# Neighbourhood attention with the values in four tiles, the division on its outputs, and fewer passes in the pooling beside it

## The chip, the cores and the metric

The kernel runs on one core of a Trainium2 chip. Its time is the device time of one execution in microseconds, from runs that are repeated on the same core. Engines are named as in the profile: PE (TensorE; PEld is its weight load), DVE (VectorE), ACT (ScalarE), POOL (GpSimd) and SP (SyncE, which here issues nearly all DMAs, one after another). PE's granted clock is given as a share of its upper level, 2.4 GHz; the lower level is 1.2 GHz.

## What is computed

Two layers over 1024 latent tokens (a grid of 16 rows and 64 columns) and 256 context tokens, 1024 features wide, in fp32. Each layer projects the normalised tokens into four groups of 256 features: a gated linear attention, a neighbourhood attention, a state-space scan and a pooling; each is multiplied by a gate, and one output projection adds the result to the stream. The change touches the neighbourhood attention (four heads of 64 features; a query sees 8 x 16 neighbours and all context tokens) and the pooling. Cut to what matters:

```
s_win = einsum('bhrqd,bhrikd->bhrqik', qg, k_rows) + bias      # qg already scaled
s_ctx = einsum('bhrqd,bhnd->bhrqn', qg, kch)
p = softmax(concat([s_win, s_ctx], -1))
o = einsum('bhrqik,bhrikd->bhrqd', p_win, v_rows) + einsum('bhrqn,bhnd->bhrqd', p_ctx, vch)

def centred_mean(u, w):          # w = 2, 4, 8, 16, 64 features each
    lo, hi = clip(t - w//2, 0, n), clip(t - w//2 + w, 0, n)
    return (csum[hi] - csum[lo]) / (hi - lo)
out_i = (centred_mean(g_i, w_i) - g_i) @ w_pool[i]
```

In layer 2 the context tokens have no queries of their own.

## The kernel before

The kernel is traced into one list of instructions per engine by a scheduler that takes them by priority and readiness and inserts the waits; each engine, and SP's queue of DMAs too, then runs its list in order. A buffer is a slot of a named tile; a new tile of that name waits until the old one's last reader is done.

For each layer the stages follow each other: projections and linear attention, the scan, then `na`, the neighbourhood attention, with the pooling and (in layer 1) gate projections woven into it, then the output projection `out_tiles`. fp32 products are made of two halves: a tile `hi` rounded to the matmul's format and `lo`, the rest.

`na` runs over jobs. A job is a head and a block of 128 queries, of which there are ten (two of context, eight of the grid); layer 1 has 40 jobs, layer 2 has 32. For a job, `na_scores` multiplies queries and keys into the score bank `nS` (L1331), DVE adds the bias and takes the maximum (L1338), ACT takes the exponential into `naP` and its sum into a column of `nast` (L1343), DVE takes the reciprocal (L1345) and scales all of `naP` by it (L1346). Three jobs later `na_turn` turns `naP` on PE by blocks of 128 (L1376), and ACT and DVE split the result into `naPT`, hi and lo (L1382, L1383). Two jobs form a pair; for a pair `na_values` multiplies `naPT` by the values into the half of a PSUM bank `nT` (L1398): rows 0 to 63 take hi by the values' hi plus lo by hi, rows 64 to 127 hi by the values' lo. ACT copies the upper rows (L1400, `nat`), and one DVE pass adds both into the head's output `nay` (L1412). `nT` has three buffers, shared by turns, values and pooling.

`na_head` loads a head's keys, queries and values. The values `naV` are one tile of ten blocks with one buffer (L1302, 640 KB), so the next head's load waits for the last product of the head before.

`pooling` goes in pieces of 256 tokens and 128 features (ten in layer 1, eight in layer 2), one after every fourth job. Each loads its input `pu` (L1453) and its inverse counts `piv` (L1455, one buffer), POOL forms window sums (L1457 to L1463), multiplies by the counts in two halves (L1465, L1466) and subtracts the input (L1467); PE multiplies by the weights (L1476), ACT copies out, and SP stores (L1479). `out_early` loads and multiplies the first output tiles (L376, L377) on SP and POOL before attention ends.

The modulation vector `csil`, 34 columns by four, is made once at the start on DVE (L185) and stays in a tile for the whole program.

Of the kernel before, what the change touches and what calls it, by code (L numbers as in the profile page):

```python
# [12 lines left out]
F32 = mybir.dt.float32  # L13
F32R = mybir.dt.float32r
I32 = mybir.dt.int32
AF = mybir.ActivationFunctionType
ALU = mybir.AluOpType
# [5 lines left out]
SEQ = 1024  # L23
CTX = 256
NTOK = SEQ + CTX
# [14 lines left out]
NH = '11'  # L40
NRM = 0
PS0 = 0
# [19 lines left out]
PW = 256  # L62
# [7 lines left out]
class Kernel:  # L70
# [72 lines left out]
    def load_consts(self):  # L143
        nc, c, a = self.nc, self.const, self.a
# [15 lines left out]
        self.dG = [self.dram.tile([D, NTOK], F32, name=f"dG{l}") for l in range(DEPTH)]  # L160
        self.dY = [self.dram.tile([D, NTOK], F32, name=f"dY{l}") for l in range(DEPTH)]
        self.dX = self.dram.tile([NTOK, D], F32, name="dX")
        self.dU = [self.dram.tile([NTOK, 256], F32, name=f"dU{l}") for l in range(DEPTH)]
# [9 lines left out]
    def silu_c(self):  # L173

        nc, v = self.nc, self.nc.vector
        cc, th = (self.t([128, 8, 2], "cc", 2) for _ in range(2))
        nc.sync.dma_start(cc, self.a["cc"])
        nc.scalar.activation(th, cc, AF.Tanh, scale=0.5)
        v.scalar_tensor_tensor(th, th, 1.0, cc, op0=ALU.add, op1=ALU.mult)
        v.tensor_scalar(th, th, 0.5, None, op0=ALU.mult)  # L180

        self.csil = self.const.tile([128, 4, 34], F32, name="csil")
        v.memset(self.csil, 0.0)
        for i in range(2):
            v.tensor_copy(self.csil[:, :, 32 * i:32 * i + 2], th.rearrange("p (a b) n -> p a b n", b=2)[:, :, i])  # L185

    def modulation(self, l, pieces, raws, width, psum, pool, lag=1):
# [1097 lines left out]
    def na_head(self, l, h, last):  # L1285
        nc = self.nc
# [7 lines left out]
        for piece in range(2):  # L1294
            q0 = 0 if piece == 0 else 640
            qt = self.t([128, NTOK], "naQ", 2, dtype=F32R).rearrange("p (i n) -> p i n", i=2)
            o = CTX if last and piece == 0 else 0
            for half in range(2):
                nc.sync.dma_start(qt[64 * half:64 * half + 64, :, o:].bitcast(F32), self.dQ[l][rows, :, q0 + o:q0 + 640])
            Q.append(qt)  # L1300
        V = self.t([128, 10, 128], "naV", 1, dtype=F32R)
        nc.sync.dma_start(V.bitcast(F32), self.dN[l][:, h * 128:(h + 1) * 128].rearrange("(t p) e -> p t e", p=128))  # L1302
        if h % 2 == 0:
# [82 lines left out]
    def na_values(self, l, job0, job1, last):  # L1386
        nc = self.nc
        (h, K, Q, V, yst), qb, r0, _, _, shared, PT, rest, ps = job0
        o = ps[:, 256:512]

        both = [(b, s, 0, 256) for s, b in enumerate(shared, 5 - len(shared))]
        one = [(b, 0, 128 * a, 128) for a, b in rest]
        hi = [(V[:, b, :], o, 0, s, q, n) for b, s, q, n in both + one]
        lo = [(V[:, b, 0:64], o[0:64], 1, s, q, n) for b, s, q, n in both + one]
        todo = hi[:1] + lo[:1] + hi[len(both):] + lo[1:] + hi[1:len(both)]
        for i, (w, out, part, s, q, n) in enumerate(todo):
            x = PT[:, part, s].rearrange("p a q -> p (a q)")[:, q:q + n]
            nc.tensor.matmul(out[:, q:q + n], lhsT=w, rhs=x, start=(i == 0), stop=(i == len(todo) - 1))  # L1398
# [7 lines left out]
        if NRM:  # L1406
            for i, r in enumerate((r0, job1[2])):
                nc.tensor.transpose(ps[0:64, i * 128:(i + 1) * 128], r.to_broadcast([128, 64]), self.ident)
            nc.vector.tensor_tensor(t[0:64], o[0:64], t[64:128], ALU.add)
            nc.vector.tensor_tensor(yc, view(t[0:64]), view(ps[0:64, 0:256]), ALU.mult if NRM == 1 else ALU.divide)  # L1410
        else:
            nc.vector.tensor_tensor(yc, view(o[0:64]), view(t[64:128]), ALU.add)  # L1412
# [15 lines left out]
    def pooling(self, l, last):  # L1428
# [4 lines left out]
        wb, sc = wb[:, 0:256].rearrange("p (m n) -> p m n", m=2), wb[:, 256:258]  # L1433
        nc.sync.dma_start(sc, a["pool_sc"][l])
        nc.sync.dma_start(wb, a["pool_wb"][l].rearrange("m k n -> k m n"))
        PAD = 8
# [3 lines left out]
        for (t0, t1, lo, hi) in pieces:  # L1440
            n = t1 - t0
            W = n + 2 * PAD
            for m in range(2):
# [9 lines left out]
                nc.sync.dma_start(u[:, d0:d1], self.dP[l][m * 128:(m + 1) * 128, c0:c1])  # L1453
                iv = self.t([128, PW], "piv", 1)
                nc.sync.dma_start(iv[:, :n], a["pool_inv"][:, m, t0:t1])  # L1455

# [7 lines left out]
                rr, uu = s4[:, PAD:PAD + n], u[:, PAD:PAD + n]  # L1464
                gp.tensor_tensor(s4[0:64, PAD:PAD + n], s2[0:64, PAD:PAD + n], iv[0:64, :n], ALU.mult)  # L1465
                gp.tensor_tensor(s4[64:128, PAD:PAD + n], s4[64:128, PAD:PAD + n], iv[64:128, :n], ALU.mult)  # L1466
                gp.tensor_tensor(rr, rr, uu, ALU.subtract)  # L1467
                todo.append((m, t0, n, u, rr, wb, sc))
# [63 lines left out]
    def run(self):  # L1532
# [9 lines left out]
        for l in range(DEPTH):  # L1542
# [5 lines left out]
            with self.phase("mods", True) as pool:  # L1548
                psum = self.ps2
                pm = lambda: psum.tile([128, 512], F32, tag="pm", bufs=1, name=self.nm("pm"))  # L1550
                todo = ((1, (2,)),) if last else ((0, (2,)), (1, (1, 0)))
# [45 lines left out]
def _consts():  # L1597
# [40 lines left out]
    out["id32"] = np.tile(np.eye(32, dtype=f), (4, 1))  # L1638
    inv = np.zeros((128, 2, NTOK), f)
    for wi, w in enumerate((2, 4, 8, 16)):  # L1640
        for off, n in ((0, CTX), (CTX, SEQ)):
            t = np.arange(n)
            cnt = np.clip(t - w // 2 + w, 0, n) - np.clip(t - w // 2, 0, n)
            inv[64 * (wi % 2):64 * (wi % 2) + 64, wi // 2, off:off + n] = (f(1.0) / cnt.astype(f))[None]
    out["pool_inv"] = inv
# [96 lines left out]
```

## Time and profile before

| | |
|---|---|
| time, median of 3 | 1372.81 us (1372.37 to 1374.88) |
| profiled execution | 1372.72 us, span 1370.9 us |
| mean granted clock of PE | 0.974 |
| PE, PEld busy | 1252.5 us (91%), 1009.2 us (74%) |
| DVE, ACT, POOL busy | 913.4 us (67%), 582.7 us (43%), 202.8 us (15%) |
| scaling of `naP` on DVE (L1346, 128x640 and 128x512) | 33.6 us for 48 and 10.0 us for 16 |

The span runs from the first to the last instruction. A busy share over the whole span mixes stages with different limits; the stage in question is read by a table of windows, and what an engine waited for by the table of waits. A wait for several things is put down to the one that came last.

### The profile page before, as it was taken

The page shows a single profiled execution, that of the slowest core. Times are in us where ns is not written, and L with a number is a line of the kernel's source. Part 1 is how long each engine was busy: PE and PEld are TensorE (multiplying, and loading weights), DVE is VectorE, ACT ScalarE, POOL GpSimd, SP SyncE. Part 2 cuts the span into 40 slices and gives each one's busy share as a digit, 9 for nine tenths or more (in the row PEclk, how much of TensorE's full clock was granted, in tenths as well). Part 3 has the DMA queues.
Part 4 walks back from the last instruction along what each step waited for, and adds up shares of the span by engine and source line. Part 5 has one row for each costly group of instructions (what it writes and reads, how often), then busy time and mean ns, then how long its engine had stood idle before and what let it go on. Part 6 is the DMA issues. An engine that isn't in the chain of part 4 may idle for free. (4 is left out here: it accounts for less than half of the span.)

```text
span 1370.9 us, 20412 instructions
## 1 busy us (share of the span) xinstructions
PE 1252.5 (91%) x7102; PEld 1009.2 (74%) x7102; DVE 913.4 (67%) x2269; ACT 582.7 (43%) x1234; POOL 202.8 (15%) x218
## 2 busy tenths in 40 slices
PE   5799999999999999888989999999999989787897
PEld 2698967676777677777778989868767766666676
DVE  2778577546388658774875689596554884877383
ACT  2653433223333347653455642453323333665321
POOL 0100000001100024442410000000212100335220
PEclk9799999999999999999999999999999999989999
DMA  9446686752533277637742475975315434864662
GB/s 330 170 124 223 195 252 177 227 161 77 166 125 117 79 195 187 179 121 234 236 117 91 134 221 187 256 200 165 88 50 184 154 127 145 213 146 131 197 209 89
DMA packets 233846, 228.99 MB, mean 167 GB/s; under 512 B 47144, under 2 KB 196136, under 8 KB 233408
## 3 DMA queue, kind: packets, MB, share of 16 engines
q1 hardware_dynamic: 232144, 225.05, 54.4%
q10 hardware_dynamic: 1584, 2.49, 0.5%
q8 instruction: 59, 0.97, 0.3%
q14 instruction: 59, 0.48, 0.1%
HBM read 157.88 MB, written 69.62 MB: 166 GB/s over the span
## 5 line engine op out<-in xcount | busy, mean ns | idle before, releaser
L317 PE MATMUL pa<-ahi,wh 128*128 128x512 f32 (+1 forms) x664 | 172.3, 386 | 3.3 <-DVE stg L346 1.5
L317 PE MATMUL pa<-ahi,wl 128*128 128x512 f32 (+1 forms) x664 | 165.9, 378 | 0.1
L317 PE MATMUL pa<-alo,wh 128*128 128x512 f32 (+1 forms) x664 | 163.8, 377 | 0.3 <-PEq L1571 0.3
L317 PEld LDWEIGHTS pa<-ahi,wh 128*128 128x128 f32 x664 | 115.4, 192 | 28.5 <-issue 6.0
L317 PEld LDWEIGHTS pa<-alo,wh 128*128 128x128 f32 x664 | 115.8, 192 | 22.5 <-issue 4.7
L317 PEld LDWEIGHTS pa<-ahi,wl 128*128 128x128 f32 x664 | 114.3, 190 | 22.7 <-issue 5.6
L302 POOL TENSOR_TENSOR wl<-w,wh 128x1024 fp32r<-128x1024 f32 (+1 forms) x19 | 46.4, 2445 | 277.7 <-PE pa L317 177.2
L333 PE MATMUL pa<-wh,ahi 128*128 128x256 f32 (+1 forms) x480 | 79.5, 300 | 4.9 <-DVE ahi L260 3.9
L387 PE MATMUL po<-wx,ahi 128*128 128x512 f32 x312 | 79.1, 393 | 2.8 <-DVE stg L473 1.6
L301 ACT CAST wh<-w 128x1024 fp32r<-128x1024 f32 (+1 forms) x51 | 53.8, 1056 | 62.5 <-PE pa L317 39.6
L333 PE MATMUL pa<-wl,ahi 128*128 128x256 f32 (+1 forms) x480 | 79.4, 299 | 0.1
L333 PE MATMUL pa<-wh,alo 128*128 128x256 f32 (+1 forms) x480 | 77.2, 296 | 0.0
L333 PEld LDWEIGHTS pa<-wh,ahi 128*128 128x128 f32 x480 | 66.8, 194 | 10.1 <-issue 3.0
L387 PEld LDWEIGHTS po<-wx,ahi 128*128 128x128 f32 x312 | 58.8, 190 | 16.3 <-ACT ahi L379 2.0
L333 PEld LDWEIGHTS pa<-wl,ahi 128*128 128x128 f32 x480 | 67.5, 194 | 3.6 <-issue 2.5
L333 PEld LDWEIGHTS pa<-wh,alo 128*128 128x128 f32 x480 | 66.2, 193 | 3.3 <-issue 3.0
L1331 PE MATMUL nS<-naK,naQ 128*128 128x256 f32 (+1 forms) x272 | 57.6, 333 | 11.4 <-DVE nast L1338 6.6
L1398 PE MATMUL nT<-naPT,naV 128*128 128x256 f32 (+3 forms) x368 | 58.1, 298 | 9.9 <-DMA naV<-dN 9.2
L1338 DVE CUSTOM_DVE_ANT_0 naP<-nS,nab 128x640 f32<-128x640 f32 (+1 forms) x64 | 50.2, 785 | 18.7 <-PE nS L1331 13.8
L1398 PEld LDWEIGHTS nT<-naPT,naV 128*128 128x128 f32 (+1 forms) x368 | 49.6, 176 | 15.4 <-issue 7.7
L1376 PE MATMUL nT<-c_ident,naP 128*128 128x128 f32 x320 | 51.5, 286 | 9.4 <-DVE nay L1412 3.9
L1383 DVE TENSOR_TENSOR naPT<-nT,naPT 128x512 fp32r<-128x512 f32 (+1 forms) x104 | 56.2, 559 | 5.7 <-ACT naPT L1382 5.3
(396 smaller groups left out, 2550.5 us busy)
## 6 DMA issues: line engine op xcount, KB each, us to landing
w<-in_w_in_dram SPq DMA_DIRECT2D x41, 512.0 KB
wm<-in_w_mod_dram SPq DMA_DIRECT2D x32, 512.0 KB
s5R<-dR SPq DMA_DIRECT2D x16, 960.0 KB
xt<-in_tok_dram SPq DMA_DIRECT2D x20, 512.0 KB
wm<-in_w_mod_dram SPq DMA_DIRECT2D x8, 1024.0 KB
dR<-sp_R SPq DMA_DIRECT2D x16, 512.0 KB
dG<-stg SPq DMA_DIRECT2D x32, 256.0 KB
w<-in_w_out_dram SPq DMA_DIRECT2D x16, 512.0 KB
```

What stands on the lines that cost most here:

```text
L301: nc.scalar.copy(hi, raw)
L302: (next(engines) if engines else self.eng(2)).tensor_tensor(lo, raw, hi.bitcast(F32), ALU.subtract)
L317: nc.tensor.matmul(ps[:, :t1 - t0], lhsT=w(k), rhs=x[:, k, t0:t1], start=(i == 0), stop=(i == 23))
L333: nc.tensor.matmul(ps[:, :n], lhsT=x[:, k, t * 128:(t + 1) * 128], rhs=w(k), start=(i == 0), stop=(i == 23))
L387: self.nc.tensor.matmul(o, lhsT=x[:, k], rhs=m(k), start=first and i == 0, stop=last and i == len(todo) - 1)
L1331: nc.tensor.matmul(self.na_s[:, c * 128:(c + n) * 128], lhsT=Qb[:, i, :], rhs=K[:, b * 128:(b + n) * 128], start=(i == 0), stop=(i == 1))
L1338: v.tensor_tensor_reduce(P[:, 0:nk], ps, self.na_b[:, b0:b0 + nk], 1.0, -NEG, ALU.add, ALU.min, nm)
L1376: nc.tensor.transpose(ps[:, i * 128:(i + 1) * 128], P[:, c * 128:(c + 1) * 128], self.ident)
L1383: (nc.gpsimd if RLO == "p" and len(src) < 4 else nc.vector).tensor_tensor(lo, pv, hi.bitcast(F32), ALU.subtract)
L1398: nc.tensor.matmul(out[:, q:q + n], lhsT=w, rhs=x, start=(i == 0), stop=(i == len(todo) - 1))
```

## The change

- The values of a head are four tiles: `naVc` for the two context blocks (two buffers), `naVa`, `naVb`, `naVd` for three, two and three blocks of the grid (one buffer each), with four loads.
- `naP` is no longer scaled. The reciprocal of each job's sum is turned on PE, as a 128x64 broadcast column against the identity, into the other half of the pair's `nT` bank, ahead of the value products. DVE adds the two halves of the output into `nat` (64x256) and a second pass multiplies by the turned reciprocals into `nay`.
- The pooling keeps 17 columns of factors per feature half, loaded once per layer: eight for the first and eight for the last tokens, made by POOL on 64x8 strips where a piece has such an edge, and the constant 1/w. DVE does the multiplication by 1/w and the subtraction in one pass for each half of 64 features.
- `csil` is stored to DRAM at the start and loaded again in the stage of each layer that uses it, so its tile is not held between.

```
-NRM = 0
+NRM = 1
+        self.dC = self.dram.tile([128, 4, 34], F32, name="dC")
-        self.csil = self.const.tile([128, 4, 34], F32, name="csil")
+        self.csil = self.t([128, 4, 34], "csil", 1)
...
+        nc.sync.dma_start(self.dC, self.csil)
...
-        V = self.t([128, 10, 128], "naV", 1, dtype=F32R)
-        nc.sync.dma_start(V.bitcast(F32), self.dN[l][:, h * 128:(h + 1) * 128].rearrange("(t p) e -> p t e", p=128))
+        parts = ((0, 2, "naVc", 2), (2, 3, "naVa", 1), (5, 2, "naVb", 1), (7, 3, "naVd", 1))
+        V = {}
+        for b, n, tag, bufs in parts:
+            x = self.t([128, n, 128], tag, bufs, dtype=F32R)
+            nc.sync.dma_start(x.bitcast(F32), self.dN[l][b * 128:(b + n) * 128, h * 128:(h + 1) * 128].rearrange("(t p) e -> p t e", p=128))
+            V.update((b + i, x[:, i]) for i in range(n))
...
         todo = hi[:1] + lo[:1] + hi[len(both):] + lo[1:] + hi[1:len(both)]
+        if NRM:
+            for i, r in enumerate((r0, job1[2])):
+                nc.tensor.transpose(ps[0:64, i * 128:(i + 1) * 128], r.to_broadcast([128, 64]), self.ident)
         for i, (w, out, part, s, q, n) in enumerate(todo):
...
         if NRM:
-            for i, r in enumerate((r0, job1[2])):
-                nc.tensor.transpose(ps[0:64, i * 128:(i + 1) * 128], r.to_broadcast([128, 64]), self.ident)
             nc.vector.tensor_tensor(t[0:64], o[0:64], t[64:128], ALU.add)
             nc.vector.tensor_tensor(yc, view(t[0:64]), view(ps[0:64, 0:256]), ALU.mult if NRM == 1 else ALU.divide)
...
+        iv = self.t([128, 2, 17], "piv", 1)
+        nc.sync.dma_start(iv, a["pool_inv"])
...
-                iv = self.t([128, PW], "piv", 1)
-                nc.sync.dma_start(iv[:, :n], a["pool_inv"][:, m, t0:t1])
...
-                gp.tensor_tensor(s4[0:64, PAD:PAD + n], s2[0:64, PAD:PAD + n], iv[0:64, :n], ALU.mult)
-                gp.tensor_tensor(s4[64:128, PAD:PAD + n], s4[64:128, PAD:PAD + n], iv[64:128, :n], ALU.mult)
-                gp.tensor_tensor(rr, rr, uu, ALU.subtract)
+                for p, x in ((slice(0, 64), s2), (slice(64, 128), s4)):
+                    for c, w, there in ((PAD, 0, t0 == lo), (PAD + n - 8, 8, t1 == hi)):
+                        if there:
+                            gp.tensor_tensor(x[p, c:c + 8], x[p, c:c + 8], iv[p, m, w:w + 8], ALU.mult)
+                    nc.vector.scalar_tensor_tensor(rr[p], x[p, PAD:PAD + n], iv[p, m, 16:17], uu[p], op0=ALU.mult, op1=ALU.subtract)
...
+                self.csil = self.t([128, 4, 34], "csil", 1)
+                nc.sync.dma_start(self.csil, self.dC)
```

The scheduler's order follows. In SP's list of layer 2, around the loads of the third head, it read before (`naQ`, `naK` queries and keys, `nab` bias, `w` output weights, `pu` and `dY<-pu` the pooling's input and output):

```order
L1453 DMA pu_18073<-dP_107 128x272
L1293 DMA naK_18212<-dK_101 64x1280 x2
L1479 DMA dY_90<-pu_17934 128x256
L1231 DMA nab_17612<-in_na_bias_dram 128x256
L1455 DMA piv_18203<-in_pool_inv_dram 128x256
L1302 DMA naV_17956<-dN_97 128x10x128
L1453 DMA pu_18199<-dP_107 128x272
L1299 DMA naQ_18215<-dQ_99 64x2x384 x2
L1415 DMA dY_90<-nay_17632 64x1024
```

and reads now:

```order
L1308 DMA naVa_18002<-dN_98 128x3x128
L1233 DMA nab_17650<-in_na_bias_dram 128x256
L1490 DMA dY_90<-pu_17853 128x256
L1308 DMA naVb_18004<-dN_98 128x2x128
L1295 DMA naK_18260<-dK_102 64x1280
L1463 DMA pu_18125<-dP_108 128x272
L1295 DMA naK_18260<-dK_102 64x1280
L1308 DMA naVd_18006<-dN_98 128x3x128
L1233 DMA nab_17650<-in_na_bias_dram 128x256
L1490 DMA dY_90<-pu_17981 128x256
L1301 DMA naQ_18263<-dQ_100 64x2x384 x2
L1463 DMA pu_18250<-dP_108 128x272
```

The one load of values stood behind a load of counts; now it is four loads, of which three are in these rows, each with other loads and stores between, and no load of counts is among them.

In DVE's list of layer 2, around the second pair of the first head, it read before (ISA is the bias and maximum pass of L1338 with the row that reads its result):

```order
L1346 TENSOR_SCALAR naP_17745<-naP_17745,nast_17746 128x640
L1383 TENSOR_TENSOR naPT_17733<-nT_17773,naPT_17733 128x128
L1345 RECIPROCAL nast_17782<-nast_17782 128x1
L1383 TENSOR_TENSOR naPT_17787<-nT_17788,naPT_17787 128x4x128
L1346 TENSOR_SCALAR naP_17781<-naP_17781,nast_17782 128x640
L1338 ISA naP_17799,nast_17800<-nS_17618,nab_17612 128x512
L1338 ISA nast_17800 128x1
L1412 TENSOR_TENSOR nay_17632<-nT_17773,nat_17831 64x2x16x8
L1383 TENSOR_TENSOR naPT_17787<-nT_17834,naPT_17787 128x4x128
L1345 RECIPROCAL nast_17800<-nast_17800 128x1
L1383 TENSOR_TENSOR naPT_17787<-nT_17841,naPT_17787 128x256
```

and reads now:

```order
L1390 TENSOR_TENSOR naPT_17834<-nT_17835,naPT_17834 128x4x128
L1355 RECIPROCAL nast_17830<-nast_17830 128x1
L1345 ISA naP_17846,nast_17847<-nS_17656,nab_17650 128x512
L1345 ISA nast_17847 128x1
L1417 TENSOR_TENSOR nat_17878<-nT_17821,nat_17878 64x256
L1478 SCALAR_TENSOR_TENSOR ps_3784_17855<-ps_3783_17854,piv_17725,pu_17853 64x256
L1478 SCALAR_TENSOR_TENSOR ps_3784_17855<-ps_3784_17855,piv_17725,pu_17853 64x256
L1355 RECIPROCAL nast_17847<-nast_17847 128x1
L1418 TENSOR_TENSOR nay_17676<-nat_17878,nT_17821 64x2x16x8
L1390 TENSOR_TENSOR naPT_17834<-nT_17882,naPT_17834 128x4x128
L1390 TENSOR_TENSOR naPT_17834<-nT_17889,naPT_17834 128x256
```

The scalings of `naP` are gone; the pass that adds into `nat` is followed by the two pooling passes and a reciprocal before the pass that multiplies into `nay` and frees the bank `nT_17821`.

On PE, the products of one pair in the same layer, with the turns of the reciprocals (`nast`) in front, read now:

```order
L1487 MATMUL nT_18389<-ps_3836_18127,pwb_17723 128x256
L1405 MATMUL nT_18357<-c_ident,nast_18223 64x128
L1405 MATMUL nT_18357<-c_ident,nast_18242 64x128
L1408 MATMUL nT_18357<-naPT_18315,naVa_18002 128x256
L1408 MATMUL nT_18357<-naPT_18315,naVa_18002 64x256
L1408 MATMUL nT_18357<-naPT_18315,naVa_18002 128x128
L1408 MATMUL nT_18357<-naPT_18315,naVa_18002 64x256
L1408 MATMUL nT_18357<-naPT_18315,naVc_18000 64x256 x2
L1408 MATMUL nT_18357<-naPT_18315,naVa_18002 64x128
L1408 MATMUL nT_18357<-naPT_18315,naVa_18002 128x256
L1408 MATMUL nT_18357<-naPT_18315,naVc_18000 128x256 x2
```

The two turns come before the first product and behind the pooling's product of that piece; before, the pair began with the product 128x256.

## Rows read from the trace of the kernel before

**Rows 1.** The page's part 1: busy us (share of the span) xinstructions.

```profile
PE 1252.5 (91%) x7102; PEld 1009.2 (74%) x7102; DVE 913.4 (67%) x2269; ACT 582.7 (43%) x1234; POOL 202.8 (15%) x218
```

**Rows 2.** Windows, attention of both layers: length, busy us (x) by engine, clock, DMA.

```profile
496.00:612.00 116.00, 103.46 (x673) 86.28 (x671) 94.67 (x233) 76.64 (x183) 50.88 (x67) 1.00 0.65 173
1165.00:1271.00 106.00, 81.24 (x490) 67.72 (x490) 81.73 (x197) 64.15 (x152) 41.48 (x56) 0.91 0.62 159
1170.00:1210.00 40.00, 31.28 (x211) 25.53 (x212) 35.62 (x91) 28.61 (x68) 12.55 (x17) 1.00 0.81 200
1210.00:1230.00 20.00, 17.25 (x93) 15.27 (x93) 14.23 (x36) 11.29 (x27) 8.65 (x12) 0.74 0.48 123
1240.00:1250.00 10.00, 4.18 (x22) 3.29 (x21) 5.50 (x13) 3.96 (x9) 4.67 (x8) 0.89 0.67 195
```

**Rows 3.** Waits, 1165 to 1300 us: engine line <- releaser: total us, times, longest.

```profile
PEld nS L1331 <- DVE nast L1338: 10.5, 18, 1.5
...
PE nT L1398 <- DMA naV<-dN: 6.1, 3, 4.4
```

**Rows 4.** Chain, 1231 to 1249 us: start us, us, what.

```profile
1242.07 0.73 POOL ps L1466
1242.82 0.33 SPq L1455
1243.21 5.24 DMA naV<-dN
```

**Rows 5.** Waits, 490 to 620 us.

```profile
PE nT L1398 <- DMA naV<-dN: 3.1, 2, 2.4
```

**Rows 6.** Lines by shape, 1165 to 1300 us: xcount | busy us, mean ns | idle.

```profile
L1346 DVE TENSOR_SCALAR naP<-naP,nast 128x640 f32<-128x640 f32 x24 | 14.9, 622 | 0.4
...
L1467 POOL TENSOR_TENSOR ps<-ps,pu 128x256 f32<-128x256 f32 x8 | 6.4, 802 | 0.6
...
L1465 POOL TENSOR_TENSOR ps<-ps,piv 64x256 f32<-64x256 f32 x8 | 6.1, 757 | 0.6
...
L1466 POOL TENSOR_TENSOR ps<-ps,piv 64x256 f32<-64x256 f32 x8 | 6.0, 745 | 0.6
...
L1346 DVE TENSOR_SCALAR naP<-naP,nast 128x512 f32<-128x512 f32 x8 | 5.4, 676 | 0.1
```

**Rows 7.** Lines by shape, 490 to 620 us.

```profile
L1376 PE MATMUL nT<-c_ident,naP 128*128 128x128 f32 x168 | 26.6, 278 | 3.6 <-DVE nay L1412 1.9 <-DVE nast L1345 1.0 <-DVE naP L1346 0.6
...
L1346 DVE TENSOR_SCALAR naP<-naP,nast 128x640 f32<-128x640 f32 x24 | 18.7, 777 | 0.2
...
L1346 DVE TENSOR_SCALAR naP<-naP,nast 128x512 f32<-128x512 f32 x8 | 4.6, 579 | 0.1
...
L1346 DVE TENSOR_SCALAR naP<-naP,nast 128x256 f32<-128x256 f32 x8 | 2.8, 354 | 0.5
```

**Rows 8.** Lines by shape, DVE, whole span.

```profile
L1412 DVE TENSOR_TENSOR nay<-nT,nat 64x256 f32<-64x256 f32 x36 | 15.0, 417 | 21.3 <-ACT nat L1400 20.6
...
L824 DVE SCALAR_TENSOR_TENSOR s5y<-s5y,s5g 128x256 f32<-128x256 f32 x2 | 0.8, 424 | 1.9 <-ACT s5y L823 1.9
```

**Rows 9.** Line 1376, what its engine waited for: us in total, times.

```profile
  DVE nay L1412: 12.9, 29
```

**Rows 10.** Timeline, 3 to 6 us: start us, us, engine line op.

```profile
4.01 1.67 SPq L211 DMA_DIRECT2D wm<-in_w_mod_dram  x3
...
5.13 0.25 DVE L185 COPY csil<-cc 128x8 f32<-128x8 f32 x2
```

**Rows 11.** Lines 1346, 380 and 1412 by themselves: duration ns min/median/max.

```profile
L1346 DVE TENSOR_SCALAR naP<-naP,nast x72: 352/550/1617, 495.8 to 1260.5; 128x640 f32<-128x640 f32 x48, 128x512 f32<-128x512 f32 x16, 128x256 f32<-128x256 f32 x8
...
L380 DVE TENSOR_TENSOR alo<-yt,ahi x28: 412/684/1790, 640.0 to 1322.7; 128x512 fp32r<-128x512 f32 x24, 128x256 fp32r<-128x256 f32 x4
...
L1412 DVE TENSOR_TENSOR nay<-nT,nat x36: 416/417/419, 507.5 to 1271.8; 64x256 f32<-64x256 f32 x36
```

More of the change, by code (lines that the diff above doesn't have):

```diff
@@ L1392, in na_values @@
         one = [(b, 0, 128 * a, 128) for a, b in rest]
-        hi = [(V[:, b, :], o, 0, s, q, n) for b, s, q, n in both + one]
-        lo = [(V[:, b, 0:64], o[0:64], 1, s, q, n) for b, s, q, n in both + one]
+        hi = [(V[b], o, 0, s, q, n) for b, s, q, n in both + one]
+        lo = [(V[b][:, 0:64], o[0:64], 1, s, q, n) for b, s, q, n in both + one]
         todo = hi[:1] + lo[:1] + hi[len(both):] + lo[1:] + hi[1:len(both)]
+        if NRM:
+            for i, r in enumerate((r0, job1[2])):
+                nc.tensor.transpose(ps[0:64, i * 128:(i + 1) * 128], r.to_broadcast([128, 64]), self.ident)
         for i, (w, out, part, s, q, n) in enumerate(todo):
@@ L1638, in _consts @@
     out["id32"] = np.tile(np.eye(32, dtype=f), (4, 1))
-    inv = np.zeros((128, 2, NTOK), f)
+    inv = np.zeros((128, 2, 17), f)
+    t = np.r_[0:8, SEQ - 8:SEQ]
     for wi, w in enumerate((2, 4, 8, 16)):
[L1641 to L1644, printed above, removed]
+        cnt = np.clip(t - w // 2 + w, 0, SEQ) - np.clip(t - w // 2, 0, SEQ)
+        at = inv[64 * (wi % 2):64 * (wi % 2) + 64, wi // 2]
+        at[:, 0:16], at[:, 16] = w * (f(1.0) / cnt.astype(f)), 1.0 / w
     out["pool_inv"] = inv
```

## The prediction

> **What bounds the kernel now.** I read the engines' sums first, then tables by stage, then the waits and the chain inside the two attention stages. Over the whole span TensorE (PE) is busy 1252.5 us of 1370.9, DVE 913.4 [rows 1]. That is an average; the change touches almost only the neighbourhood attention, once per layer, so I cut those two stages out [rows 2]: layer 1 at 496 to 612 us, layer 2 at 1165 to 1271 us. They differ. In layer 1 gate projections fill the gaps and PE is busy 103.5 of 116 us; DVE 94.7. In layer 2 little filler is left: PE 81.2 of 106 us, DVE 81.7, and between 1170 and 1210 us, where nothing stalls, DVE has 35.6 of 40 us and PE only 31.3. There DVE sets the pace: the loads of the score weights wait 10.5 us in all for the DVE pass that frees the score banks [rows 3]. Behind that stretch come two holes. In 1240 to 1250 us PE has 4.2 of 10 us; in 1210 to 1230 us it is busy, but at a granted clock of 0.74 [rows 2].
>
> The holes have a cause in the chain [rows 4]: the second of POOL's multiplications by the inverse counts ends at 1242.8 us, only then can SP issue the next load of those counts (one buffer), and only behind that the one load of all values of the next head, which lands 5.24 us later. SP issues in order, so POOL's pace holds attention's loads. PE waits for the values 6.1 us in layer 2 [rows 3] and 3.1 us in layer 1 [rows 5].
>
> **The change, part by part.** The rows' own execution took 1372.72 us (span 1370.9 and 1.8 around it), beside a median of 1372.81: the sum can start from either.
>
> *Values in four tiles.* The single buffer is free only after the head's last product, so the load cannot be hidden. Now the context blocks have two buffers and the other tiles come free one or two query pairs before they are wanted (the order rows of SP show them spread out, among other loads). A pair lasts 106/16 = 6.6 us, the whole load took 5.24 [rows 4], a quarter of it should take less. I take the waits as gone: -6.1 in layer 2, -3.1 in layer 1. Bounds: nothing (the new loads wait on PE in SP's queue and delay the queries behind them), and -9.2. What is late next is the pooling input and the queries, which stand in the same queue.
>
> *Division on the outputs.* Removed: 32 scalings of P in layer 2, 14.9 + 5.4 = 20.3 us [rows 6], and 40 in layer 1, 18.7 + 4.6 + 2.8 = 26.1 us [rows 7]. Added on DVE: one more 64x256 pass per pair, which the present one prices at 0.417 us [rows 8], so 16 x 0.417 = 6.7 and 20 x 0.417 = 8.3 us. Added on PE: two turns per pair. The trace has no 64x128 turn; the nearest is the 128x128 one, 26.6 us for 168 or 0.158 us [rows 7]. I take that: 32 x 0.158 = 5.1 us and 40 x 0.158 = 6.3 us. Ends: 0, if they fall into idle PE, and the whole 11.4.
>
> *Shorter pooling.* 18 loads of counts become 2, so SP no longer waits for POOL there; that gain is already in the waits for values. POOL loses 757 + 745 + 802 ns per piece [rows 6] and gets a few 64x8 products, which cost nothing while POOL is busy 41.5 of 106 us [rows 2]. DVE gets two 64x256 passes per piece. Nearest row: a scalar_tensor_tensor of 256 elements at 0.424 us [rows 8], so 16 x 0.424 = 6.8 us in layer 2 and 20 x 0.424 = 8.5 in layer 1. At a stage's end, where the last piece is waited for, 2.30 us of POOL give way to 0.85 of DVE and two edge products: I take -1.1 in layer 2 and -1.0 in layer 1; ends -1.5 and +0.9, a piece held once by DVE's queue.
>
> DVE net: layer 2 -20.3 + 6.7 + 6.8 = -6.8; layer 1 -26.1 + 8.3 + 8.5 = -9.3.
>
> *What of this reaches the path.* In layer 2 DVE paces most of the stage, so I count 5 of the 6.8. PE has a quarter of the stage idle, so its 5.1 count 1.5. In layer 1 PE is 89% busy: of the 9.3 from DVE I count 3, but of PE's 6.3 more than half, 3.5.
>
> *What waits longer.* The bank with a pair's outputs is freed by the last DVE pass on it. Now that is the second pass, and the order rows of DVE show other work between the two (a pooling pair, a reciprocal). Queued behind it on PE are the turns of the next job, and behind those ACT and the splitting passes. Today these turns wait for that DVE pass 29 times, 12.9 us in all [rows 9]. One pass more on every pair is 15.0 us (the price of rows 8 times 36); zero if DVE, relieved, comes to it earlier. I take +2.5 in layer 2 and +2.0 in layer 1. The turns of the sums themselves stand ahead of the products and need only a reciprocal that is long done.
>
> *The rest.* The modulation vector moves through DRAM: one store and two loads. The store waits at the start for DVE's copies, which end at 5.38 us, and the second weight load is queued behind it, while today three go out within 1.67 us from 4.01 [rows 10]. I cost it at 0, since the first loads are still on their way then; at most it is 1.3 us, from about 4.5 us to the 5.8 at which the store is out. The clock: 20 us at 0.74 are 5.2 us of full-speed work lost [rows 2]; with fewer holes I take back 1.
>
> **Sum.** Layer 2: -6.1 - 5.0 - 1.1 + 1.5 + 2.5 = -8.2. Layer 1: -3.1 - 3.0 - 1.0 + 3.5 + 2.0 = -1.6. Clock -1.0. Together -10.8: 1372.7 - 10.8 = 1361.9, so 1362 us.
>
> **A rule against it.** The removed scaling ran 352 to 1617 ns, and a splitting pass with both inputs in SBUF 412 to 1790 ns, while the pass over PSUM and SBUF kept to 416 to 419 [rows 11]. So passes of the first kinds are held by something, and the two new pooling passes read two SBUF operands. The Trainium skill, "SBUF — State Buffer", section "Who interferes with whom", says that a DVE instruction with two SBUF inputs and a GpSimd instruction that reads SBUF exclude each other for the whole instruction. The spreads agree with it. By that rule the passes that go (2-port scalings) were victims as well, so it cuts both ways; only the rival below takes it at its worst.
>
> **Rivals.**
> *The larger gain.* Layer 2 drops to its engines' own work. PE 81.2 less 106 x 0.09 = 9.5 for the slow clock plus 5.1 is 76.8 us, DVE 81.7 - 6.8 = 74.9. At the 0.89 share that DVE holds in the undisturbed stretch the stage takes 76.8 / 0.89 = 86.3 us, 19.7 less than 106; layer 1 as PE-bound gains nothing: 1353 us. For it: both holes have one cause. Against: the chain leaves other loads late.
>
> *No change.* Each of the 36 new pooling passes is held by one POOL product (0.745 us, rows 6), 26.8 us on DVE; the net of -16.1 becomes +10.7. The 8 us counted for DVE are gone and some 3 come on top: 1361.9 + 11 = 1373 us. For it: the spreads. Against: POOL is left with about 41.5 - 18.4 = 23 us in 106, so a pass meets it one time in five.
>
> *Slower: the output bank held over two passes.* Place: the turns of the next job, in both layers. Price per pair 0.417 us, and 0.85 more where the pooling pair stands between the passes, which happens for up to 18 of the 36. With PE's 11.4 in full and the removed waits at -9.2 - 2.1 = -11.3 these two cancel, and if DVE's freed time stays unused, every delayed pair counts: half of them, 18 x 0.417 = 7.5, give 1380 us. It decides as soon as more than 10 pairs are held without DVE's gain. For it: 29 such waits today. Against: each of them is short (0.44 us), and DVE is what gets relieved.
>
> **How the numbers follow.** The forecast 0.56, the larger gain 0.20, no change 0.11, slower 0.13. A measurement of this kernel tells about 0.2%, 2.7 us. Faster by more than that: nearly all of the first two and a little of the third, 0.76; within: 0.11; slower: 0.13. The forecast's own range is 1355 to 1369; with the larger gain's lower end and the no-change case 1348 to 1375, which leaves out most of the slower case.
>
> **What would show it.** In the changed profile no matmul of values should wait for a load by more than about a microsecond; the stretch of layer 2's attention should be 7 to 11 us shorter and its clock nearer 1; the turns of the sums should be near 0.16 us of PE each; the waits of turns for the second output pass should stay under 18 us in all; layer 1's stage should be within 3 us of 116. I am wrong if PE's idle time in layer 2 stays near 25 us under another releaser (pooling, queries, the output pass), or if layer 1's stage grows by more than 3 us.

## The result, and the profile after

The changed kernel is slower: 1386.11 us median (1380.85 to 1390.71, 7 runs) beside 1372.37 (1370.91 to 1374.88, 7 runs) of the kernel before, a ratio of 1.0095 with a 95% interval of 1.0077 to 1.0114. My 1362 us is off by 24, and the result lies above the range (1348 to 1375).

The engines' sums of the profiled run (1388.17 us, span 1386.4) answer to [rows 1]:

```profile
PE 1252.4 (90%) x7174; PEld 1013.0 (73%) x7174; DVE 912.8 (66%) x2269; ACT 583.4 (42%) x1234; POOL 165.0 (12%) x188
```

PE and DVE do as much as before, POOL 38 us less, and the span is 15.5 us longer. The loss is idle time: PE has 134.0 us of it where it had 118.4. Windows of the same lengths as the attention stages in [rows 2], with the same columns, begun within 3 us of the first score product:

```profile
498.00:614.00 116.00, 103.43 (x670) 87.45 (x669) 84.57 (x218) 72.40 (x175) 25.45 (x46) 0.97 0.57 153
1180.00:1286.00 106.00, 80.06 (x520) 67.98 (x521) 78.29 (x196) 63.89 (x149) 23.51 (x40) 0.94 0.57 151
```

PE is idle for 25.9 of 106 us in layer 2, as before (24.8), but its releaser is another one. These are waits of the changed kernel, 1175 to 1288 us (engine line <- releaser: us in total, times, longest):

```profile
POOL ps L1465 <- DMA pu<-dP: 43.5, 4, 16.1
PEld nS L1338 <- DVE nast L1345: 23.0, 21, 4.3
...
PE nS L1338 <- DVE nast L1345: 17.2, 12, 4.1
```

The wait for values [rows 3] has gone; the load of the score weights waits 23.0 us for DVE's bias/max pass (L1345, formerly L1338) where it was 10.5. Over the whole span, the instructions that write the score bank `nS` wait for that pass so long (us, times), first in the kernel before, then in the changed one. Each sum counts the weight loads and the products, which in part wait at the same time; the line below it has PE's products alone, which wait 14.9 us more than before:

```profile
  DVE nast L1338: 22.7, 47
PE nS L1331 <- DVE nast L1338: 6.6, 13, 1.3
```

```profile
  DVE nast L1345: 54.1, 54
PE nS L1338 <- DVE nast L1345: 21.5, 16, 4.1
```

Why is DVE late at it, with less work? The changed kernel's chain (start us, us, what), then DVE, POOL and PE in order of time around it:

```profile
1225.97 3.64 DMA dY<-pu
...
1229.66 4.62 DMA pu<-dP
...
1234.45 0.65 POOL ps L1465
...
1235.16 0.64 POOL ps L1469
...
1235.87 0.64 POOL ps L1470
...
1236.54 1.04 DVE ps L1478
1237.58 0.03 issue
1237.62 0.48 DVE ps L1478
...
1238.13 0.82 DVE naP L1345
...
1239.02 1.43 PE nS L1338 x4
```

```profile
1234.78 0.42 DVE L1417 TENSOR_TENSOR nat<-nT,nat 64x256 f32<-64x256 f32 x1 [0.66 <-ACT nat L1410]
1236.54 1.56 DVE L1478 SCALAR_TENSOR_TENSOR ps<-ps,piv,pu 64x256 f32<-64x256 f32 x2 [1.35 <-POOL ps L1470]
1238.13 0.82 DVE L1345 CUSTOM_DVE_ANT_0 naP<-nS,nab 128x640 f32<-128x640 f32 x1
```

```profile
1236.58 0.72 POOL L1471 TENSOR_TENSOR ps<-ps 64x256 f32<-64x256 f32 x1
```

```profile
1239.02 1.43 PE L1338 MATMUL nS<-naK,naQ 128*128 128x384 f32 x4 [4.08 <-DVE nast L1345]
...
1247.44 0.59 PE L1487 MATMUL nT<-ps,pwb 128*128 128x256 f32 x2
```

Read it from the top: a finished pooling output is stored from `pu`; only then may the same buffer be loaded for a later piece; POOL sums it; the two new DVE passes need the sums; the next bias/max pass stands behind them in DVE's list; and PE needs that one before it writes the next scores. PE stands still for 4.08 us. Up to 2.9 of them, from the end of DVE's pass before (1234.78 + 0.42) to the bias/max pass, are the wait for POOL and the two passes, for a piece of pooling whose product PE multiplies at 1247.44. Before, POOL waited for `pu` as much, but alone; its waits over the whole span, in the kernel before and in the changed one:

```profile
POOL ps L1457 <- DMA pu<-dP: 65.7, 12, 14.1
```

```profile
POOL ps L1465 <- DMA pu<-dP: 53.9, 7, 16.1
```

### The profile page after: what moved, and what is told of

Same layout as the page of the kernel before. It is cut to its first block, busy times and chain, and to the rows that moved or that the text cites. A ratio compares the mean times of both kernels' runs of the same rounds, so it can differ in the third digit from the quotient of the medians.

```text
span 1386.4 us, 20596 instructions
## 1 busy us (share of the span) xinstructions
PE 1252.4 (90%) x7174; PEld 1013.0 (73%) x7174; DVE 912.8 (66%) x2269; ACT 583.4 (42%) x1234; POOL 165.0 (12%) x188
## 5 line engine op out<-in xcount | busy, mean ns | idle before, releaser
L319 PE MATMUL pa<-ahi,wl 128*128 128x512 f32 (+1 forms) x664 | 170.2, 382 | 0.0
L319 PE MATMUL pa<-alo,wh 128*128 128x512 f32 (+1 forms) x664 | 160.6, 374 | 0.3 <-PEq L1584 0.3
L1338 PE MATMUL nS<-naK,naQ 128*128 128x256 f32 (+1 forms) x272 | 59.2, 339 | 25.3 <-DVE nast L1345 21.5
L335 PE MATMUL pa<-wl,ahi 128*128 128x256 f32 (+1 forms) x480 | 76.6, 294 | 0.1
L1338 PEld LDWEIGHTS nS<-naK,naQ 128*128 128x128 f32 x272 | 41.7, 198 | 39.6 <-DVE nast L1345 32.6
L1350 ACT ACTIVATE naP<-naP,nast 128x640 f32<-128x640 f32 (+1 forms) x64 | 51.5, 805 | 28.2 <-DVE nast L1345 22.0
L348 DVE SCALAR_TENSOR_TENSOR stg<-stg,pa 128x512 f32<-128x512 f32 (+1 forms) x40 | 25.2, 631 | 50.2 <-ACT stg L347 46.8
```

The lines of the kernel that those rows point to most:

```text
L319: nc.tensor.matmul(ps[:, :t1 - t0], lhsT=w(k), rhs=x[:, k, t0:t1], start=(i == 0), stop=(i == 23))
L335: nc.tensor.matmul(ps[:, :n], lhsT=x[:, k, t * 128:(t + 1) * 128], rhs=w(k), start=(i == 0), stop=(i == 23))
L348: nc.vector.scalar_tensor_tensor(th[:, :t1 - t0], th[:, :t1 - t0], 1.0, ps, op0=ALU.add, op1=ALU.mult)
L1338: nc.tensor.matmul(self.na_s[:, c * 128:(c + n) * 128], lhsT=Qb[:, i, :], rhs=K[:, b * 128:(b + n) * 128], start=(i == 0), stop=(i == 1))
L1350: nc.scalar.activation(P[:, 0:nk], src, AF.Exp, bias=nm, scale=-1.0, accum_out=l1)
```

## The experiments

In their names the three digits say whether the values are in four tiles, the pooling passes on DVE, the division on the outputs; 111 is the change. All have the small table of counts, and all but `e_table` the stored `csil`. Ratios are against the kernel before on the same chip, with 95% intervals. "Layer 1" is the time from its first score product to its first output product, "layer 2" that from its last projection to the end, each from one profile (143.0 and 206.2 us before, 151.7 and 209.3 in the change), so that differences of two or three us are not read.

**One part undone.** Pooling passes back on POOL:

```diff
-                    nc.vector.scalar_tensor_tensor(rr[p], x[p, PAD:PAD + n], iv[p, m, 16:17], uu[p], op0=ALU.mult, op1=ALU.subtract)
+                    gp.tensor_tensor(rr[p], x[p, PAD:PAD + n], iv[p, m, 16:17].to_broadcast([64, n]), ALU.mult)
+                gp.tensor_tensor(rr, rr, uu, ALU.subtract)
```

> The changed kernel (1386.1 us) with the pooling passes off DVE again: POOL multiplies each half by its count and subtracts the input, out of the small table; the values in four tiles and the division on the outputs stay. Theory 1 (DVE's queue: the 36 pooling passes stand in DVE's list ahead of bias/max passes and wait there for POOL, and so for the load of `pu`; on the chain of layer 2's attention `pu` loads and L1478 hold some 7 us each): the wait of PE's score products for the bias/max pass falls from 54 us back to about 23, and the time to 1360 to 1368. Rival 2 (the division on the outputs is what costs: the 72 turns and the bank held over two passes): 1380 to 1386. Rival 3 (the four value loads hold up SP's queue): 1380 to 1386.

Division back on the probabilities (`NRM = 0`):

> The changed kernel with the division put back on the probabilities (72 scalings of naP on DVE, one output pass, no turns of the sums); values in four tiles and DVE's pooling passes stay. Theory 1 (DVE waits in its queue for the pooling sums): DVE gets some 20 us of scalings in each layer's attention and loses 7 us of output passes, and still waits for POOL, so no better than 1386, up to 1400. Rival 2 (the division on the outputs costs): 1368 to 1378.

One value tile again (`naV`, ten blocks, one load):

> The changed kernel with the values in one tile and one load a head again. Theory 1: the value waits of 6.1 us in layer 2 and 3.1 us in layer 1 come back, in part under the waits of DVE: 1386 to 1395. Rival 3 (four loads on SP, each held until PE gives its tile free, delay the loads of `pu` and queries behind them): 1372 to 1380.

Two of the three undone (the first edit, and `NRM = 0`):

> Only the values in four tiles (and, as in all these kernels, the small table of counts and `csil` stored and loaded again): scalings on the probabilities, pooling all on POOL. Theory 1: the value waits of the kernel before (9.2 us in both layers) go and about half of it shows, 1366 to 1370 against 1372.4 before. Rival 3 (the four loads are what cost): 1378 to 1386.

Measured: e101 0.9955 (0.9934 to 0.9977), e110 1.0037 (1.0016 to 1.0059), e011 1.0099 (1.0065 to 1.0133), e100 0.9929 (0.9902 to 0.9957). Taking the passes off DVE is worth 1.4% (19 us) with the division on the outputs and 1.1% (15 us) without. The wait for the bias/max pass falls from 54.1 to 32.3 us in e101, not to the 23 of the text. With the scalings that wait is the same with the passes on DVE (24.4 us, e110) and without (24.6, e100); there PE's products of the pooling wait 12.1 us where it was 5.1, so that the loss shows at another place of PE's list. The value tiles gain nothing while DVE stalls (1.0099 without them against 1.0095), so four loads in SP's queue are not what costs. e110 speaks against theory 1 as the only cause: that had said no gain, and it gained 0.6%, so the division on the outputs costs too. Its 1379.87 us lie just above rival 2's 1368 to 1378, its ratio within them (1.0037 of 1372.4 is 1377.5). e100 is a little faster than its text, which had not counted the small table.

**The other combinations.** The same edits, combined:

> Values in one tile and pooling all on POOL; of the change only the division on the outputs with its turns is left (and the small table, and `csil` stored and loaded). From the runs so far: taking DVE's pooling passes out was worth 1.4% with the values split (0.9955 against 1.0095), so theory 1 expects 0.996 to 1.000 here against 1.0099 with the passes. If the passes cost only together with the split values (their loads between those of `pu` in SP's queue), 1.005 to 1.010.

> None of the three parts: scalings on the probabilities, one tile of values, pooling on POOL; only the small table of counts (17 columns, loaded once a layer, with edge passes) and `csil` stored and loaded twice. All theories: 0.997 to 1.002 of before. If the trip of `csil` delays the gated stages, 1.002 to 1.004; if the small table's fewer loads on SP help by themselves, 0.993 to 0.997.

> The kernel before with only the small table of counts: one load a layer in the place of 18 of 128 KB, the edges multiplied by POOL apart, the rest by one number a row, still on POOL; `csil` stays in its tile. With `csil` moved as well it was 0.9959. If the table is the gain and the trip of `csil` costs nothing: 0.994 to 0.998. If the table gives nothing: 0.999 to 1.001.

Measured: e001 1.0008 (0.9992 to 1.0024), e000 0.9959 (0.9934 to 0.9985), e_table 0.9964 (0.9943 to 0.9985). e001 lies just above what was expected, e000 on the table's side: the small table alone gives 0.4%, and nothing shows that moving `csil` costs. The split values give 0.3% (e000 to e100), within its uncertainty of 0.4, and 0.5% (e001 to e101), clear of its 0.3; the division on the outputs costs 0.3 to 0.6% in three pairs, each uncertain by some 0.3.

**Wait or work?** The DVE passes with their shape and their place in the list, but no POOL to wait for, in the kernel with one value tile:

```diff
-                    nc.vector.scalar_tensor_tensor(rr[p], x[p, PAD:PAD + n], iv[p, m, 16:17], uu[p], op0=ALU.mult, op1=ALU.subtract)
+                    nc.vector.scalar_tensor_tensor(pd[p, :n], pd[p, :n], self.na_r[p], pd[p, :n], op0=ALU.mult, op1=ALU.subtract)
```

Here `pd` is a tile of ones and `na_r` the latest reciprocal. For the first 128 features POOL also forms its last sum on 128 rows instead of 64.

> The one-tile kernel with DVE's 36 pooling passes of the same shape and place in DVE's list, but on a tile of their own and the reciprocal just before them, so that they wait for no POOL and no load (PE then takes the plain window sums: the counts and the subtraction are left out of the output). Theory 1a (the wait in DVE's queue is what costs): near the kernel with pooling on POOL, 0.996 to 1.001 of before. Theory 1b (the DVE time itself, 36 passes of some 0.4 to 0.6 us on the loop score bank, bias/max pass, next scores): 1.005 to 1.010, as with the wait.

A third buffer for the pooling input:

```diff
-                u, s2, s4 = (self.t([128, PW + 2 * PAD], x, b) for x, b in (("pu", 2), ("ps2", 1), ("ps4", 2)))
+                u, s2, s4 = (self.t([128, PW + 2 * PAD], x, b) for x, b in (("pu", 3), ("ps2", 1), ("ps4", 2)))
```

> The one-tile kernel with DVE's pooling passes as in the change, but three buffers for `pu`, so that a piece's load no longer waits for the store of the piece two before. Theory 1a: POOL's wait for `pu` (89 us in all with one tile) falls by half or more, DVE's passes find their sums ready, 1.000 to 1.004 of before. Theory 1b: 1.007 to 1.010, no change from 1.0099.

Measured: e011_nowait 0.9920 (0.9891 to 0.9950), e011_pu3 1.0002 (0.9981 to 1.0023), against 1.0099 for e011. These are the passes (xcount | busy us, mean ns | idle before) of e011, of e011_pu3, and of e011_nowait:

```profile
L1475 DVE SCALAR_TENSOR_TENSOR ps<-ps,piv,pu 64x256 f32<-64x256 f32 x36 | 21.6, 600 | 21.1 <-POOL ps L1474 11.9 <-POOL ps L1467 4.7 <-POOL ps L1462 3.8
```

```profile
L1475 DVE SCALAR_TENSOR_TENSOR ps<-ps,piv,pu 64x256 f32<-64x256 f32 x36 | 21.7, 603 | 16.3 <-POOL ps L1474 8.2 <-POOL ps L1467 5.9 <-POOL ps L1462 1.0
```

```profile
L1478 DVE SCALAR_TENSOR_TENSOR pd<-pd,nast 64x256 f32<-64x256 f32 x36 | 18.9, 526 | 0.4
```

18.9 us of work stay on DVE, the 21.1 us of waiting go, and the kernel is 1.8% (24 us) faster: theory 1b, the passes' own time, had said 1.005 to 1.010. But the 24 us are not the price of the wait alone. The kernel is faster than either range of its text, and 0.9% faster than e001, which has no such passes on DVE at all. The edit also frees POOL's tiles earlier, and PE's products of the pooling need neither POOL's multiplications nor DVE's passes: they wait 2.3 us, where it was 7.1 in e011 and 9.1 in e001. The mended kernels below do without this edit. Earlier loads give 1.0% (13 us): they shorten DVE's wait (21.1 to 16.3 us), POOL's wait for `pu` falls from 89.5 to 70.3 us and not by half, and PE's products of the pooling wait no more.

**The whole change, mended.** The passes stand one pooling step later, tied to that step's reciprocal so that the scheduler can't pull them forward; first with the tiles of the change, then with three `pu` and one buffer for the context values, then that with the division on the probabilities:

```diff
...
+                if late:
+                    w = self.t([128, 1], "pw", 2)
+                    nc.vector.tensor_scalar(w, self.na_r, 0.0, late[0][2], op0=ALU.mult, op1=ALU.add)
+                    for p, o, x, y in late[1:]:
+                        nc.vector.scalar_tensor_tensor(o, x, w[p], y, op0=ALU.mult, op1=ALU.subtract)
+                late = [(0, 0, iv[:, m, 16:17])]
                 if len(todo) == PLAG:
...
-                    nc.vector.scalar_tensor_tensor(rr[p], x[p, PAD:PAD + n], iv[p, m, 16:17], uu[p], op0=ALU.mult, op1=ALU.subtract)
+                    late.append((p, rr[p], x[p, PAD:PAD + n], uu[p]))
...
```

The small pass into `w` multiplies the reciprocal by zero and adds the constant 1/w, so that it can't run before that reciprocal. The passes of a layer's last piece stand behind all others, without that tie.

> All three parts of the change, but each piece's two DVE passes stand one pooling step (four jobs) later in DVE's list, behind a small pass of one column that ties them to that step's reciprocal; `pu` keeps two buffers. Theory 1a (the wait of DVE's passes for POOL and the load of `pu` is what made the change slower): the sums are ready four jobs, about 13 us, after the load is due, most of the wait goes, 0.990 to 0.998 of before. If a piece's load is late by more than those 13 us (it still waits for the store of the piece two before), the wait only moves: 1.000 to 1.008.

> As the one before, with three buffers for `pu` and one for the first two value blocks (memory for both there is not). Theory 1a: 0.987 to 0.995 of before, DVE's waits for POOL near 0 and the score products' wait for the bias/max pass below 35 us; 1b (DVE's own time): no better than 1.000.

> As e111_fix3 with the division back on the probabilities. The division on the outputs has cost 0.3 to 0.6% in the three pairs so far. If that cost is PE's 72 turns and the bank held over two passes, this kernel is 0.983 to 0.991 and below e111_fix3; if DVE, now with 20 us more of scalings and the pooling passes, becomes the bound, it is above e111_fix3, 0.992 to 1.000.

Measured: e111_fix2 0.9944 (0.9917 to 0.9970), e111_fix3 0.9939 (0.9913 to 0.9965), e110_fix3 0.9988 (0.9963 to 1.0012). In e111_fix3 the 32 moved passes wait for nobody, POOL waits for them instead (68.9 us in all, and the kernel is faster in spite of it), and the score bank's wait (second fence) is that of the kernel with pooling on POOL:

```profile
L1459 DVE SCALAR_TENSOR_TENSOR ps<-ps,pw,pu 64x256 f32<-64x256 f32 x32 | 17.4, 544 | 0.7
```

```profile
  DVE nast L1345: 32.4, 48
```

All three parts of the change with the passes moved are 1.5% (21 us) faster than the change, and faster than before. In e111_fix2 nothing else differs from the change but the 16 small passes into `w`: the 36 passes are still on DVE, and the values, turns and second passes are as they were. With the scalings in the place of the division on the outputs (e110_fix3) the kernel is 0.5% slower than e111_fix3 (uncertain by 0.4), as the text had it for a DVE that becomes the bound: here the division on the outputs gains.

**The division on the outputs.** Without the turns (the second pass multiplies by the product bank, as in the edit below), without the second pass, without both; in e001, with pooling on POOL. All three leave the division by the sums out:

```diff
-        if NRM:
-            for i, r in enumerate((r0, job1[2])):
-                nc.tensor.transpose(ps[0:64, i * 128:(i + 1) * 128], r.to_broadcast([128, 64]), self.ident)
...
-            nc.vector.tensor_tensor(yc, view(t[0:64]), view(ps[0:64, 0:256]), ALU.mult if NRM == 1 else ALU.divide)
+            nc.vector.tensor_tensor(yc, view(t[0:64]), view(o[0:64]), ALU.mult if NRM == 1 else ALU.divide)
```

> The kernel with the division on the outputs alone (1.0008), without the 72 turns of the sums on PE: the second output pass multiplies by the product bank in the place of the turned reciprocals, so the outputs are not divided by the sums. If the turns are the cost (13.8 us of PE in both layers, in layer 1 beside the gate projections with PE at its limit): 0.994 to 0.997, at or below the kernel with the scalings (0.9959). If the second pass and the bank held for it are the cost: 0.999 to 1.001.

> The division on the outputs alone (1.0008), without the second output pass on DVE; the 72 turns of the sums stay on PE, nobody reads them, and the outputs are not divided. If the turns are what the division on the outputs costs: 0.999 to 1.001. If the second pass and the bank held for it are: 0.993 to 0.997.

> No division at all: neither the 72 scalings nor the turns nor the second output pass (the outputs are not divided by the sums); one tile of values, pooling on POOL. It shows what the removal of the scalings is worth by itself, against 0.9959 with them. If the 45 us of scalings stood half on the path, as I forecast: 0.978 to 0.986. If they ran beside PE, ACT and the loads, which set the pace: 0.993 to 0.997.

Measured: e001_noturn 0.9983 (0.9958 to 1.0008), e001_onepass 0.9984 (0.9963 to 1.0005), e001_nodiv 0.9890 (0.9857 to 0.9924), beside 0.9959 with scalings and 1.0008 with turns and second pass. So the 45.4 us of scalings are worth 0.7%, 9.5 us, less than half and more than nothing (0.9890 lies between the two ranges of its text), and what replaces them costs 1.2%, 16 us. Turns alone cost 0.9%, the second pass alone 0.9%, both together 1.2%: neither of the two texts in noturn and onepass came true, and how the cost divides stays open, since each of these differences is uncertain by some 0.4%.

In layer 1 PE is the busiest engine. Windows from the first score product to the first output product of e001, then of e000:

```profile
496.50:639.00 142.50, 133.45 (x834) 112.96 (x833) 89.19 (x228) 86.11 (x199) 53.73 (x89) 0.98 0.59 164
```

```profile
495.30:633.00 137.70, 128.61 (x794) 108.44 (x794) 105.99 (x249) 86.28 (x199) 56.15 (x88) 0.99 0.61 169
```

PE is busy 93 to 94% of the stretch in both; its work grows by 4.8 us (40 more matmuls) and the stretch by 4.8, though DVE has 16.8 us less to do. That looks as if the turns lay on the path there, but other profiles don't bear it out: the stretch is 141.5 us in e001_noturn, without turns, and 135.8 in e011_nowait, with them. In layer 2 the scalings seem to count: 209.0 us in e000, 199.2 in e001_nodiv, though e000's profiled execution took 1372.26 us, 5 above its median. Hence the last kernel, with the values split, pooling on POOL, and the outputs divided in layer 2 alone (its text counts layer 2 otherwise; as counted here, its two values are 202.8 and 199.4):

```diff
     def na_scores(self, l, job, last):
+        NRM = int(last)
...
     def na_values(self, l, job0, job1, last):
+        NRM = int(last)
```

> Values in four tiles, pooling on POOL, and the division on the outputs in layer 2 alone. The profiles so far: in layer 1, where PE also has the gate projections, the division on the outputs lengthens the stretch from the first score to the first output product (139.5 us without, 141.9 with, values split; 137.7 and 142.5 with one tile); in layer 2 it shortens the stretch from the last projection to the end (193.4 without, 190.1 with). If that is right, 0.988 to 0.992, below 0.9929 with scalings in both layers and 0.9955 without. If the two layers do not differ: 0.993 to 0.996.

Measured: 0.9905 (0.9873 to 0.9937), 1360.74 us beside 1373.15: faster than before and than the change. It is 0.5% (uncertain by 0.4) under e101, which divides in both layers, so the division on the outputs costs in layer 1. Its interval overlaps that of e100 (0.9929), so that dividing in layer 2 is better than not dividing is likely, not shown.

## Why the prediction was wrong

*The step that failed is the shorter pooling.* I priced the passes on DVE by their length, 6.8 and 8.5 us, and as to waiting let the term end at +0.9: "a piece held once by DVE's queue". Their length was mis-sized a little (604 ns instead of 424, 21.8 us in all over both layers); what I left out is that they wait in DVE's list for POOL, and POOL for a load that waits for a store. The passes in the change (xcount | busy us, mean ns | idle before):

```profile
L1478 DVE SCALAR_TENSOR_TENSOR ps<-ps,piv,pu 64x256 f32<-64x256 f32 x36 | 21.8, 604 | 18.2 <-POOL ps L1477 12.0 <-POOL ps L1470 4.4 <-POOL ps L1465 0.6
```

These 18.2 us of DVE's idle time stood at nothing in my sum. Of the kernel's time the passes cost 12 to 19 us by the three pairs with and without them, and where they stood cost 21 us by the kernel that only moves them (e111_fix2). I had written that the pooling input would be late next, and put that with SP's queue and the values; POOL's waits for `pu`, 65.7 us in the trace of before, belonged to this step, and the question was who would now stand behind POOL. As the Trainium skill says in "PSUM — Partial Sum Buffer", section "Engine vs sequencer instructions", DVE's queue is strictly first in, first out; the chain above agrees, with 1.35 us of waiting in front of a bias/max pass that was not tied to it.

*The division on the outputs* was mis-sized too, second in size. My sum had 8.0 us of gain on DVE, with the pooling passes already taken off, and 5.0 of PE and 4.5 of the held bank against it. Removing the scalings by itself is worth 9.5 us in all. I had weighed the layers the right way, a loss in layer 1 and a small gain in layer 2; e10m against e101 has the loss at some 7 us (uncertain by 5), where my three terms for layer 1 make 2.5. And I priced the turn like the 128x128 one at 0.158 us. The changed kernel's turns, by line (xcount | busy us, mean ns | idle before):

```profile
L1405 PE MATMUL nT<-c_ident,nast 128*64 128x128 f32 x72 | 14.5, 284 | 4.7 <-DVE naPT L1390 3.1 <-DMA naQ<-dQ 1.3
```

That is 0.20 us each, 14.5 us where I had 11.4, of which I let 5.0 count. With the second pass they cost 16.

*Values in four tiles*: no value product of the change waits for a load, where it was 9.2 us, but that is mostly not the tiles' doing. I had said that with one buffer the load cannot be hidden; with one tile and the small table alone the products wait 0.8 us (e_table), and with `csil` moved as well not at all (e000). The loads of counts that kept SP waiting for POOL [rows 4] were the cause of these waits. The tiles' own gain, 4 to 7 us with pooling on POOL, does not show while DVE stalls; where it comes from is open in the pair with scalings, in which neither kernel waits for values (in e001 PE's products do, 3.6 us).

*The small table* gave 0.4%, 5 us: I had booked SP's freed queue under the values and gave the table by itself 2.1 us.

In one order of putting the parts in (e000, e100, e101, the change) the measured steps are -5.6 us for the table and `csil`, -4.1 for the tiles, +3.6 for the division and +19.2 for the passes on DVE (each uncertain by 3 to 5), where my sum had -10.8 for all of it.

*The bank held over two passes*, my rival on the slower side, was not the cause. What the turns of `naP` wait for, in the change (us, times; 12.9, 29 in [rows 9]):

```profile
  DVE nay L1418: 3.4, 3
```

PE's products of the pooling, which use the same buffers, wait for that pass another 5.8 us, and the two together are still less than before.

*The rival of no change* had the DVE passes held by POOL at 27 us on DVE, through a shared port. DVE was held by about this much (21.8 us of passes and 18.2 of waits for 15.3 of forecast work), but mostly in the list. My own signs of error came true: PE idle near 25 us in layer 2 under another releaser, and layer 1 (first score to last output pass) 133.8 us where it had been 122.5.

## What to carry to other kernels

Before an operation is moved to an engine, ask not only for its time there but for what it waits for, and what stands behind it in that engine's list: an operand that was harmlessly late on an engine nobody waits for is a stall on the one that sets the pace. If it must go there, put it behind the wait (a step later, with the buffers for that), not at the place where its data are made. And a saving counts by what else is full: the division on the outputs cost in layer 1, where PE is the busiest, and gained where DVE had the scalings and the moved passes together.

## What the runs showed of the hardware

A pooling pass on DVE, both tensor operands in SBUF, takes 465 ns at least, 485 as a median and up to 1918 in the change. The pair at 1236.54 us above took 1.56 us, with a POOL sum running beside from 1236.58 to 1237.30; in layer 2, four pairs with no POOL sum beside took 0.99 to 1.04, two of them beside a 64x8 product of 0.2 us. This agrees with the exclusion that the prediction cites from the Trainium skill, and it costs half a microsecond in three of layer 2's eight pieces, and some 4.3 us over all 36 passes (21.8 less 36 x 0.485): a small part of the loss. POOL's multiplication by one number a row took 609 ns in layer 2 of e101, where the one by the full table took 757 and 745 [rows 6]. Over the whole span the medians are 610 against 732 and 728, and 611 in e_table, which has the scalings on DVE as before:

```profile
L1478 POOL TENSOR_TENSOR ps<-ps,piv 64x256 f32<-64x256 f32 x16 | 9.7, 609 | 1.2
```
